# Where a weight buffer lies in 256 bytes: whi 64 bytes before x, wlo at x

## The chip, the cores and the metric

One core of a Trainium2 chip runs the whole program. The metric is the device time of one execution in microseconds (us), as the median of several runs; lower is better. The profile is of one execution on the chip. Its engines are PE (TensorE, matmuls), PEld (the weight loads of the same engine, which overlap the matmuls), DVE (VectorE), ACT (ScalarE), POOL (GpSimd) and SP (SyncE, which issues most DMAs).

## The reference

Two layers of a decoder trunk on x of 256 positions by 2048 features in float32, then a last RMSNorm. Most of the arithmetic is in the projections; the mixers between them are small beside these.

```python
for l in range(DEPTH):                              # DEPTH = 2
    h = rms_norm(x, norm_mix[l])
    proj = h @ w_in[l]                              # 2048 -> 6656
    hq, hf, hi, hg, rq, rk, rv, rg, aq, ak, av = jnp.split(proj, split_at, axis=-1)
    mixed = jnp.concatenate([
        hgrn2_mixer(hq, hf, hi, hg, lb_all[l]),     # gated linear recurrence, 4 heads
        retention_mixer(rq, rk, rv, rg, cos, sin),  # 4 heads
        dilated_attention(aq, ak, av, rel_bias),    # 8 heads, three dilations
    ], axis=-1)
    x = x + mixed @ w_out[l]                        # 2048 -> 2048
    u = rms_norm(x, norm_ffn[l])
    gate = causal_dwconv(u @ w_gate[l], conv_w[l], conv_b[l])   # 2048 -> 5504, width 3
    x = x + (jax.nn.silu(gate) * (u @ w_up[l])) @ w_down[l]     # 5504 -> 2048
return rms_norm(x, norm_final)
```

## The kernel before, in words

**Two parts of each number.** To multiply float32 numbers with the faster float32r matmul, the kernel splits every operand into a first part (hi, the number as ACT writes it in float32r) and a second part (lo, what is left, made by DVE's subtraction). A product is then hi by hi, hi by lo and lo by hi.

**Units.** The weights are cut into units of 128 partitions x 1024 columns (512 KB), 788 in all, walked through in one list. For each unit `dma_unit` (L153) brings the float32 weights into a tile `raw` by a DMA of SP, seven units ahead; `split_unit` (L162) makes `whi` on ACT (recorded at the helper's line, L122) and `wlo` on DVE (L170), three units ahead; `mm_unit` (L173) does the matmuls. `raw` has five buffers in turn, `whi` and `wlo` four each.

**Two modes.** In mode B (w_in in part, w_out, w_gate, w_up, w_down) the weights are stationary, 128 columns at a time, and x streams. A tile of x holds, for each of two blocks of 128 features, 256 columns of hi and then 256 of lo, so the matmul with whi streams all 512 and the one with wlo the first 256. Such two matmuls are called a pair. In mode A (the other part of w_in) a piece of x is stationary and 512 columns of whi or wlo stream, in groups of three matmuls:

```python
# mode B, L202 and L203: out, stationary, streamed
nc.tensor.matmul(o, hi[:, w], x, start=first, stop=False, skip_group_check=True)
nc.tensor.matmul(o[:, 0:S], lo[:, w], x[:, 0:S], start=False, stop=last, skip_group_check=True)
# mode A, L209 to L211
nc.tensor.matmul(o, xh, hi[:, w], start=first, stop=False)
nc.tensor.matmul(o, xh, lo[:, w], start=False, stop=False)
nc.tensor.matmul(o, xl, hi[:, w], start=False, stop=last)
```

Each matmul in the code is two records in the profile: a LDWEIGHTS on PEld, which brings the stationary operand into the array, and a MATMUL on PE, which streams the other one. The x of a unit is in `hp` (the normed x of w_in, w_gate and w_up, built by `build_h`), in `mixp` (the mixers' outputs, for w_out) or in `actp` (the FFN's inner values, for w_down).

**Where the tiles lie.** A pool lays its tags one behind the other in the order in which they are first asked for, each with as many buffers as it has. In `wpool` that is raw, whi, wlo, with 4096 bytes a partition in each buffer. Behind it come `mpool`, which holds all the buffers of x (4096 bytes each, eight for hp, 22 slots that mixp, actp and the mixers' values share, and some smaller tiles of 1024 or 2048), and `const` with xt (4 x 4096), cst (1024), par (1728), masks (1024) and ones (512), in this order. `ones` is the stationary operand of the sums of squares (L273, L1038, L1093).

**Order.** The list of units, and with it the order of PE's matmuls, is written out in `layer`. Small generators (`steps`) put the mixers, the norms and the evacuations between the units; the main loop lets them go on after each unit by about 1.25 us of DVE and 1.3 us of ACT.

Of the kernel before, what the change touches and what calls it, by code (L numbers as in the profile page):

```python
# [10 lines left out]
F32 = mybir.dt.float32  # L11
F32R = mybir.dt.float32r
# [4 lines left out]
P = 128  # L17
# [65 lines left out]
def hybrid_kernel(ctx: ExitStack, tc: tile.TileContext, io):  # L83
    nc = tc.nc

    wpool = ctx.enter_context(tc.tile_pool(name="wpool", bufs=4))
# [33 lines left out]
    def act(out, in_, fn, **kw):  # L120
        want(fn)
        nc.scalar.activation(out, in_, fn, **kw)  # L122
# [30 lines left out]
    def dma_unit(u, parts=1, between=None):  # L153
# [5 lines left out]
                between()  # L159
        raws[u] = t  # L160

    def split_unit(u, parts=1):  # L162
        r = raws.pop(u)
        hi = wpool.tile([P, 1024], F32R, name=f"whi{u}", tag="whi")
        lo = wpool.tile([P, 1024], F32R, name=f"wlo{u}", tag="wlo")
        n = 1024 // parts
        for i in range(parts):
            cs = slice(i * n, (i + 1) * n)
            act(hi[:, cs], r[:, cs], AF.Copy)
            nc.vector.tensor_tensor(lo[:, cs], r[:, cs], hi[:, cs].bitcast(F32), op=OP.subtract)  # L170
        splits[u] = (hi, lo)
# [887 lines left out]
    units = []  # L1059
# [37 lines left out]
    steps.add(first_stats(), 0)  # L1097
    build_h(0, g0)
    split_unit(0, 2)
    dma_unit(3)  # L1100
    build_h(1, g0)
    split_unit(1)
    dma_unit(4)
    xin(6)
    xin(7)
    build_h(2, g0)
    build_h(3, g0)
    split_unit(2)
    dma_unit(5)
    dma_unit(6)  # L1110
# [111 lines left out]
```

## Time and profile before

| | |
|---|---|
| median of 3 runs | 2293.56 us (2293.48 to 2294.77) |
| profiled execution | 2293.8 us, span 2292.0 us |
| granted TensorE clock, mean | 0.997 |
| PE busy | 2267.9 us (99%), 12710 matmuls |
| PEld busy | 1976.2 us (86%), 12710 loads |
| DVE, ACT, POOL busy | 1512.9 us (66%), 1084.1 us (47%), 176.0 us (8%) |
| DMA | 425.10 MB, mean 185 GB/s |

A busy time is the sum of an engine's records. The ends of matmuls are modelled and overlap the next ones, so the rate of PE is read from the starts, not from the busy share. A group row reads: line, engine, operation, out<-in by tile names, shapes, xcount, then the busy us, the mean ns of one, and the engine's idle time just before them with what ended it. A timeline row reads: start and duration in us, engine, line, operation, tiles, shapes, count. A row of one line's instructions reads: the count, the shortest, median and longest duration in ns, and the first and the last start in us. A row of a stretch has its length and then the busy us (and count) of PE, PEld, DVE, ACT and POOL, the clock, the DMA share and GB/s.

### The profile page before, as it was taken

How to read it: one execution, taken by the hardware profiler on the slowest of the kernel's cores; microseconds unless marked ns; L12 is line 12 of the kernel's file. 1: busy time of each engine (PE TensorE's matmuls, PEld its weight loads, DVE VectorE, ACT ScalarE, POOL GpSimd, SP SyncE). 2: the span in 40 equal slices, each digit the busy share in tenths (PEclk: the TensorE clock that was granted, in tenths of full speed). 3: DMA queues.
4: the chain of work that ended last, by engine and by line, in shares of the span. 5: the costliest groups of instructions: out<-in, count | busy, mean ns of one | idle time of the engine just before them, and what ended most of it. 6: DMA issues, size and time to landing. Idle time of an engine off the chain costs nothing.

```text
span 2292.0 us, 32328 instructions
## 1 busy us (share of the span) xinstructions
PE 2267.9 (99%) x12710; PEld 1976.2 (86%) x12710; DVE 1512.9 (66%) x1898; ACT 1084.1 (47%) x1381; POOL 176.0 (8%) x149
## 2 busy tenths in 40 slices
PE   8999999999999999999999999999999999999997
PEld 7888888888888888888888888888888888888886
DVE  5785656777777777555558765577777777765554
ACT  5554544444444444434456444444444444444442
POOL 0250001100000000000012400020000000001111
PEclk9999999999999999999999999999999999999999
DMA  7554455555555555655555455555555555555553
GB/s 256 187 180 166 158 191 177 191 185 193 192 189 189 187 191 188 197 188 189 192 197 180 166 166 175 169 182 197 188 193 187 191 192 190 189 192 190 188 193 110
DMA packets 119587, 425.10 MB, mean 185 GB/s; under 512 B 13411, under 2 KB 16012, under 8 KB 119308
## 3 DMA queue, kind: packets, MB, share of 16 engines
q1 hardware_dynamic: 118412, 420.50, 54.6%
q10 hardware_dynamic: 1024, 2.55, 0.3%
q8 instruction: 100, 1.64, 0.3%
q14 instruction: 51, 0.42, 0.1%
HBM read 420.88 MB, written 3.68 MB: 185 GB/s over the span
## 4 chain that ended last, share of the span: by engine, by line
PE 96%; DVE 2%; POOL 1%; DMA 1%; issue 0%; ACT 0%; DVEq 0%; SPq 0%; POOLq 0%
PE acc L202 54%; PE acc L203 28%; PE acc L209 4%; PE acc L211 4%; PE acc L210 4%; DVE wlo L170 1%; DMA raw<-in_w_b 0%; PE ps_rstd L1093 0%; PE ps_qk L680 0%; DVE rt L760 0%; PE ps_o L710 0%; PE ps_pt L700 0%; PE ps_rs L793 0%; ACT whi L122 0%; POOL hx L488 0%
## 5 line engine op out<-in xcount | busy, mean ns | idle before, releaser
L170 DVE TENSOR_TENSOR wlo<-raw,whi 128x1024 fp32r<-128x1024 f32 (+1 forms) x789 | 998.7, 1269 | 723.7 <-ACT whi L122 717.3
L202 PE MATMUL acc<-hp,whi 128*128 128x512 f32 x3520 | 1230.3, 394 | 7.3 <-ACT whi L122 5.6
L122 ACT ACTIVATE whi<-raw 128x1024 fp32r<-128x1024 f32 (+1 forms) x789 | 831.4, 1056 | 809.7 <-PE acc L202 550.5
L203 PE MATMUL acc<-hp,wlo 128*128 128x256 f32 x3520 | 986.2, 280 | 0.0
L202 PEld LDWEIGHTS acc<-hp,whi 128*128 128x128 f32 x3520 | 660.3, 188 | 155.2 <-ACT whi L122 7.6
L203 PEld LDWEIGHTS acc<-hp,wlo 128*128 128x128 f32 x3520 | 666.4, 189 | 0.6 <-DVE wlo L170 0.4
L202 PE MATMUL acc<-actp,whi 128*128 128x512 f32 x1376 | 477.1, 391 | 0.0
L203 PE MATMUL acc<-actp,wlo 128*128 128x256 f32 x1376 | 385.3, 280 | 0.0
L202 PEld LDWEIGHTS acc<-actp,whi 128*128 128x128 f32 x1376 | 257.3, 187 | 56.4
L203 PEld LDWEIGHTS acc<-actp,wlo 128*128 128x128 f32 x1376 | 260.1, 189 | 0.0
L209 PE MATMUL acc<-whi,hp 128*128 128x512 f32 x448 | 181.0, 404 | 0.0
L202 PE MATMUL acc<-mixp,whi 128*128 128x512 f32 x512 | 178.9, 395 | 0.0
L248 POOL TENSOR_TENSOR sq<-xt 128x512 f32<-128x512 f32 x31 | 33.2, 1071 | 1862.1 <-DVE xt L319 1198.7
L211 PE MATMUL acc<-whi,hp 128*128 128x512 f32 x448 | 175.0, 391 | 0.0
L210 PE MATMUL acc<-wlo,hp 128*128 128x512 f32 x448 | 174.4, 389 | 0.0
L203 PE MATMUL acc<-mixp,wlo 128*128 128x256 f32 x512 | 141.9, 277 | 0.0
L202 PEld LDWEIGHTS acc<-mixp,whi 128*128 128x128 f32 x512 | 96.0, 188 | 21.8
L211 PEld LDWEIGHTS acc<-whi,hp 128*128 128x128 f32 x448 | 84.1, 188 | 18.3
L209 PEld LDWEIGHTS acc<-whi,hp 128*128 128x128 f32 x448 | 84.2, 188 | 16.7
L210 PEld LDWEIGHTS acc<-wlo,hp 128*128 128x128 f32 x448 | 84.3, 188 | 16.6
L203 PEld LDWEIGHTS acc<-mixp,wlo 128*128 128x128 f32 x512 | 96.2, 188 | 0.0
L122 ACT ACTIVATE actp<-up 128x512 fp32r<-128x512 f32 (+1 forms) x44 | 27.4, 623 | 83.3 <-DVE up L849 83.3
(195 smaller groups left out, 1177.4 us busy)
## 6 DMA issues: line engine op xcount, KB each, us to landing
raw<-in_w_d SPq DMA_DIRECT2D x172, 512.0 KB, 3.3
raw<-in_w_g SPq DMA_DIRECT2D x168, 512.0 KB, 3.2
raw<-in_w_u SPq DMA_DIRECT2D x168, 512.0 KB, 3.2
raw<-in_w_a SPq DMA_DIRECT2D x112, 512.0 KB, 3.3
raw<-in_w_b SPq DMA_DIRECT2D x95, 512.0 KB, 3.2
raw<-in_w_out SPq DMA_DIRECT2D x64, 512.0 KB, 3.5
xt<-in_x SPq DMA_DIRECT2D x8, 256.0 KB, 6.6
bias<-brow_d SPq DMA_DIRECT2D x4, 512.0 KB, 4.5
```

Source lines behind the costliest of these rows:

```text
L122: nc.scalar.activation(out, in_, fn, **kw)
L170: nc.vector.tensor_tensor(lo[:, cs], r[:, cs], hi[:, cs].bitcast(F32), op=OP.subtract)
L202: nc.tensor.matmul(o, hi[:, w], x, start=first, stop=False, skip_group_check=True)
L203: nc.tensor.matmul(o[:, 0:S], lo[:, w], x[:, 0:S], start=False, stop=last, skip_group_check=True)
L209: nc.tensor.matmul(o, xh, hi[:, w], start=first, stop=False)
L210: nc.tensor.matmul(o, xh, lo[:, w], start=False, stop=False)
L211: nc.tensor.matmul(o, xl, hi[:, w], start=False, stop=last)
L248: nc.gpsimd.tensor_tensor(sq, x, x, op=OP.mult)
```

## The change

`split_unit` asks for the tiles in another layout. A tile `lead_hi` of 48 floats (192 bytes a partition), which nothing reads or writes, is laid ahead of the buffers of whi, and a tile `lead_lo` of 16 floats (64 bytes) ahead of those of wlo. Each buffer of whi is 1088 floats instead of 1024; the 1024 in use begin at its first float where the unit's mode is B, and 16 floats (64 bytes) further where it is A. Nothing else is changed.

```diff
+    split_leads = []
+
     def split_unit(u, parts=1):
         r = raws.pop(u)
-        hi = wpool.tile([P, 1024], F32R, name=f"whi{u}", tag="whi")
+
+
+        if not split_leads:
+            split_leads.append(wpool.tile([P, 48], F32, name="lead_hi", tag="lead_hi", bufs=1))
+        skip = 0 if units[u][1][0][0].mode == "B" else 16
+        hi = wpool.tile([P, 1024 + 64], F32R, name=f"whi{u}", tag="whi")[:, skip:skip + 1024]
+        if len(split_leads) == 1:
+            split_leads.append(wpool.tile([P, 16], F32, name="lead_lo", tag="lead_lo", bufs=1))
         lo = wpool.tile([P, 1024], F32R, name=f"wlo{u}", tag="wlo")
         n = 1024 // parts
         for i in range(parts):
```

## The prediction

> **What bounds the kernel now.** I read the page's busy times and slices first, then its chain and the waits of the matmul engine, then its groups, and last the timeline and counts of single stretches.
>
> ```profile
> span 2292.0 us, 32328 instructions
> PE 2267.9 (99%) x12710; PEld 1976.2 (86%) x12710; DVE 1512.9 (66%) x1898; ACT 1084.1 (47%) x1381; POOL 176.0 (8%) x149
> PEclk9999999999999999999999999999999999999999
> PE 96%; DVE 2%; POOL 1%; DMA 1%; issue 0%; ACT 0%; DVEq 0%; SPq 0%; POOLq 0%
> ...
> L202 PE MATMUL acc<-hp,whi 128*128 128x512 f32 x3520 | 1230.3, 394 | 7.3 <-ACT whi L122 5.6
> L203 PE MATMUL acc<-hp,wlo 128*128 128x256 f32 x3520 | 986.2, 280 | 0.0
> L202 PE MATMUL acc<-actp,whi 128*128 128x512 f32 x1376 | 477.1, 391 | 0.0
> L203 PE MATMUL acc<-actp,wlo 128*128 128x256 f32 x1376 | 385.3, 280 | 0.0
> L202 PE MATMUL acc<-mixp,whi 128*128 128x512 f32 x512 | 178.9, 395 | 0.0
> L203 PE MATMUL acc<-mixp,wlo 128*128 128x256 f32 x512 | 141.9, 277 | 0.0
> ```
>
> PE is busy for 99% of the span at full clock, makes 96% of the chain, and waits for other engines for a few microseconds in all (7.3 before the largest group). So the time is how fast PE takes its own instructions. Their durations don't tell that: 394 and 280 ns overlap. The spacing of starts does, in a stretch with nothing else on PE:
>
> ```profile
> L203 PE MATMUL acc<-hp,wlo x1154: 280/280/280, 1600.0 to 1999.7; 128*128 128x256 f32 x193
> L203 PE MATMUL acc<-actp,wlo x491: 280/280/280, 2099.9 to 2269.8; 128*128 128x256 f32 x164
> ```
> ```profile
> 1699.84 0.28 PE L203 MATMUL acc<-hp,wlo 128*128 128x256 f32 x1
> 1699.95 0.39 PE L202 MATMUL acc<-hp,whi 128*128 128x512 f32 x1
> 1700.18 0.28 PE L203 MATMUL acc<-hp,wlo 128*128 128x256 f32 x1
> 1700.30 0.39 PE L202 MATMUL acc<-hp,whi 128*128 128x512 f32 x1
> ```
> ```profile
> 1699.84 0.19 PEld L202 LDWEIGHTS acc<-hp,whi 128*128 128x128 f32 x1
> 1699.95 0.19 PEld L203 LDWEIGHTS acc<-hp,wlo 128*128 128x128 f32 x1
> ```
>
> The first row holds 1153 spacings in 399.7 us, 346.7 ns a pair; the second 169.9 / 490, 346.7 again, on other x buffers. A pair is one L202 matmul of 512 columns and one L203 of 256. The timeline splits it: 0.23 us from L202 to L203 and 0.11 to 0.12 (at 230 and 116.7 ns the two make 346.7) from L203 to the next L202. The weight loads start with the matmul before: the load of wlo runs under L202's 512 columns, the load of whi under L203's 256. There are 3520 + 1376 + 512 = 5408 pairs, 5408 x 346.7 ns = 1875 us of the 2292.
>
> How much of it is surplus can be had from a second shape. Where the weights stream instead, three matmuls of 512 columns, each with a load, make a group:
>
> ```profile
> 1227.66 0.39 PE L209 MATMUL acc<-whi,hp 128*128 128x512 f32 x1
> ...
> 1228.34 0.39 PE L209 MATMUL acc<-whi,hp 128*128 128x512 f32 x1
> ```
>
> 0.68 us a group, 226.7 ns a matmul. With c ns a column and f ns a matmul, 512c + f = 226.7 and 768c + 2f = 346.7: f is 2 x (346.7 - 1.5 x 226.7) = 13.3 ns and c 0.417. So each matmul with its load costs some 13 ns beside its columns. That this part isn't a property of the shapes alone is told by another rate on the very same addresses:
>
> ```profile
> 192.01 0.40 PE L202 MATMUL acc<-hp,whi 128*128 128x512 f32 x1
> 192.24 0.28 PE L203 MATMUL acc<-hp,wlo 128*128 128x256 f32 x1
> 192.36 0.40 PE L202 MATMUL acc<-hp,whi 128*128 128x512 f32 x1
> 192.60 0.28 PE L203 MATMUL acc<-hp,wlo 128*128 128x256 f32 x1
> 192.72 0.40 PE L202 MATMUL acc<-hp,whi 128*128 128x512 f32 x1
> 192.96 0.28 PE L203 MATMUL acc<-hp,wlo 128*128 128x256 f32 x1
> 193.07 0.40 PE L202 MATMUL acc<-hp,whi 128*128 128x512 f32 x1
> ```
>
> Here three pairs take 1.06 us, 353.3 ns each, 6.7 more, though nothing waits; the L202 to L203 steps are 0.23, 0.24, 0.24 and the steps back 0.12, 0.12, 0.11. The pattern repeats for some ten microseconds. So a pair's time isn't a property of its shapes alone: how the load and the streamed operand fall against each other in time moves it. That is my reason to think that how they fall in the memory can move it too.
>
> **The change part by part.** Addresses: raw, whi, wlo and the buffers of x (hp, mixp, actp) all have sizes that are multiples of 256 bytes, so today all of them begin at the same place in 256. After it, a 192-byte lead comes ahead of whi and one of 64 ahead of wlo, and each whi is 4352 bytes (17 x 256): whi starts at 192, that is x minus 64, and wlo at 192 + 64 = 256, as x. Where the weights stream (L209 to L211) the view starts 64 bytes in, so whi is as x there.
>
> *Instructions.* None is added, removed or moved: the lead tiles are never written. No DMA, queue or wait changes, 32328 instructions stay. Cost nothing, since there is nothing to hide. The pools grow by 256 + 4 x 256 = 1280 bytes a partition.
>
> *ACT and DVE on whi.* ACT writes whi and DVE reads it, 64 bytes away from raw and wlo.
>
> ```profile
> L170 DVE TENSOR_TENSOR wlo<-raw,whi 128x1024 fp32r<-128x1024 f32 x144 | 176.4, 1225 | 108.9 <-ACT whi L122 106.4
> L122 ACT ACTIVATE whi<-raw 128x1024 fp32r<-128x1024 f32 x145 | 153.3, 1057 | 125.5 <-PE acc L202 93.2 <-issue 20.8 <-ACT conv L122 11.5
> 1600.00:2000.00 400.00, 400.00 (x2309) 352.73 (x2308) 287.97 (x361) 189.70 (x217) 0.00 (x0) 1.00 0.56 190
> ```
>
> Eight pairs, one unit, take 2774 ns of PE; DVE's 1225 and ACT's 1057 for it are made three units ahead. In the stretch DVE is busy 288 of 400 us and ACT 190. I take zero, and even 200 ns more per unit on DVE (144 x 0.2 = 29 us) would leave it below the 400. Were that cover gone, the 5408 / 8 = 676 units of this mode at 0.2 us would be 135 us.
>
> *Streaming weights (L209 to L211).* whi and wlo stay in phase with x: the 226.7 ns stay. Zero, both ways.
>
> *The load of wlo under L202.* Both stay at the same phase, so the 230 ns step stays. Zero, but for what its neighbour hands on.
>
> *The load of whi under L203.* This alone is changed, in 5408 steps of 116.7 ns. No row shows a load of this kind of tile at x minus 64. One tile does lie there: par has 1728 bytes, 64 short of 7 x 256, so ones (after masks of 1024) is at x minus 64, and it is loaded behind L203 and L211:
>
> ```profile
> 1154.50 0.28 PE L203 MATMUL acc<-hp,wlo 128*128 128x256 f32 x1
> 1154.61 0.59 PE L273 MATMUL ps_rstd<-sacc,ones 128*128 128x256 f32 x2
> ```
> ```profile
> 1565.93 0.28 PE L203 MATMUL acc<-hp,wlo 128*128 128x256 f32 x1
> 1566.05 0.59 PE L273 MATMUL ps_rstd<-sacc,ones 128*128 128x256 f32 x2
> ```
>
> 0.11 and 0.12 us: no difference that can be read, but these are single steps into a float32 matmul, not a steady row of float32r ones, and a pair shifts a few ns from one step to the next without a change of its sum. The nearest rows for the steady case are the kernel's own steps from L203 to L202 in a second pattern:
>
> ```profile
> 1500.18 0.39 PE L202 MATMUL acc<-mixp,whi 128*128 128x512 f32 x1
> 1500.41 0.27 PE L203 MATMUL acc<-mixp,wlo 128*128 128x256 f32 x1
> 1500.52 0.40 PE L202 MATMUL acc<-mixp,whi 128*128 128x512 f32 x1
> 1500.76 0.28 PE L203 MATMUL acc<-mixp,wlo 128*128 128x256 f32 x1
> ```
>
> There the step is 0.11, with 0.24 from L202 to L203 in exchange; I read it as 112.5 ns, the middle between 110 and the 115 at which it would be rounded to 0.12. Bounds: at the fast end all 13.3 ns of this one matmul go, 5408 x 13.3 = 72 us less, 2222. At the slow end the 353.3 ns pattern becomes the rule, 5408 x 6.7 = 36 us more, 2330; half of it, a step of 0.12 throughout, is 18 us more, 2312. I take 116.7 - 112.5 = 4.2 ns, the nearest row: the step that the kernel already shows, kept this time instead of exchanged. 5408 x 4.2 = 22.7 us less.
>
> Sum: the profiled execution took 2293.8 us (span 2292.0 and 1.8 around it), 0.2 above the median 2293.56. 2293.8 - 22.7 = 2271.1.
>
> **The rivals.** *Nothing happens.* The 13.3 ns are what a change of weights costs, and a shift of 64 bytes does nothing: 2293.6. For it: 346.7 to four digits on hp and on actp, and the two ones rows; against it: 353.3 ns at 192 us. [...]
>
> *The loads fall into the slow pattern.* A place 64 bytes off leaves the load of whi a little later against L203's columns, the next L202 starts late, and each pair is as at 192 us: 0.24 and 0.12. It decides once the step from L203 to L202 is above 117 ns in the long stretches. Price 36 us if all pairs fall in, 2330; 18 us if half of it, 2312. For it: the pattern exists, and holds itself for ten microseconds. Against it: today's long stretches all leave it within a few units.
>
> *The change gives much more.* Most of the 13.3 ns are a meeting of the two reads, and at x minus 64 they miss each other: down to 2222. For it: the fixed part is the same 13.3 ns in both shapes, and both read at one phase. Against it: the load of ones at x minus 64 shows nothing like it. [...]
>
> **How the numbers follow.** A measurement here tells about 0.2% (4.6 us) from no change; the three runs lie within 1.3 us. Faster 0.46: 0.38 for a part of the 13.3 ns, up to 10 (54 us, 2240), and 0.08 for more than that. Nothing: 0.29. Slower 0.25: 0.17 for up to 18 us, 0.08 above. The forecast is the likeliest, the part, at 2271; its own range is 2240 to 2288. From 2240 to 2312, 0.08 is left out at either end.
>
> **What would show it.** In the changed profile, the L203 count between 1600 and about 2000 us gives the pair: 342.5 ns if right, 346.7 for nothing, 353 for the slow pattern; the timeline there should show 0.11 from L203 to L202 and 0.23 still from L202 to L203; groups of L209 still 0.68 us; DVE's L170 near 1225 ns; 32328 instructions. I am wrong if the L202 to L203 step moves though its load didn't, or if PE begins to wait for whi or wlo.

## The result, and the profile after

The changed kernel took 2257.71 us (median of 4 runs, 2255.88 to 2258.10) against 2293.52 us: a ratio of 0.9842 with a 95% interval of 0.9825 to 0.9859, 35.8 us less. In its listing L202 and L203 (mode B) are L211 and L212, the group L209 to L211 (mode A) is L218 to L220, and L170 is L179. From its page, and from its groups between 1600 and 2000 us:

```profile
span 2255.9 us, 32328 instructions
PE 2232.3 (99%) x12710; PEld 1954.4 (87%) x12710; DVE 1512.4 (67%) x1898; ACT 1083.2 (48%) x1381; POOL 177.9 (8%) x149
PEclk9999999999999999999999999999999999999999
PE 96%; DVE 2%; POOL 1%; DMA 1%; issue 0%; ACT 0%; DVEq 0%; SPq 0%; POOLq 0%
```
```profile
L179 DVE TENSOR_TENSOR wlo<-raw,whi 128x1024 fp32r<-128x1024 f32 x148 | 181.3, 1225 | 103.1 <-ACT whi L122 101.6
L122 ACT ACTIVATE whi<-raw 128x1024 fp32r<-128x1024 f32 x147 | 155.3, 1057 | 121.5 <-PE acc L211 59.7 <-DVE conv L843 30.6 <-issue 20.0
```

The clock (0.997), the instruction counts and the chain's shares are as before (the busy shares of PEld, DVE and ACT are a point higher, as the span is shorter), and DVE's 1225 and ACT's 1057 ns are the same to the nanosecond. What has moved is the pace of PE. The counts of the matmul with wlo, and the timeline (starts in the first column):

```profile
L212 PE MATMUL acc<-hp,wlo x1177: 276/276/276, 1600.0 to 1999.9; 128*128 128x256 f32 x197
L212 PE MATMUL acc<-actp,wlo x471: 276/276/276, 2069.9 to 2229.7; 128*128 128x256 f32 x157
```
```profile
1699.75 0.39 PE L211 MATMUL acc<-hp,whi 128*128 128x512 f32 x1
1699.98 0.28 PE L212 MATMUL acc<-hp,wlo 128*128 128x256 f32 x1
1700.09 0.39 PE L211 MATMUL acc<-hp,whi 128*128 128x512 f32 x1
1700.32 0.28 PE L212 MATMUL acc<-hp,wlo 128*128 128x256 f32 x1
1700.43 0.39 PE L211 MATMUL acc<-hp,whi 128*128 128x512 f32 x1
```

399.9 us over 1176 spacings and 159.8 over 470 are 340.0 ns a pair, where it was 346.7. 5408 pairs times 6.67 ns are 36.1 us, and the span fell by 2292.0 - 2255.9 = 36.1: the whole gain is there. At 192 us, where the kernel before took 353.3 ns a pair, the changed one is at 340 too (1.02 us for three pairs):

```profile
192.21 0.39 PE L211 MATMUL acc<-hp,whi 128*128 128x512 f32 x1
...
193.23 0.39 PE L211 MATMUL acc<-hp,whi 128*128 128x512 f32 x1
```

In mode A, twelve matmuls lie between these two starts, 2.72 / 12 = 226.7 ns each, unchanged:

```profile
1217.70 0.39 PE L220 MATMUL acc<-whi,hp 128*128 128x512 f32 x1
...
1220.42 0.39 PE L220 MATMUL acc<-whi,hp 128*128 128x512 f32 x1
```

### The profile page after: what moved, and what is told of

Read it like the earlier page. It is cut to its first block, busy times and chain, and to the rows that moved or that the text cites. A ratio compares the mean times of both kernels' runs of the same rounds, so it can differ in the third digit from the quotient of the medians.

```text
span 2255.9 us, 32328 instructions
## 1 busy us (share of the span) xinstructions
PE 2232.3 (99%) x12710; PEld 1954.4 (87%) x12710; DVE 1512.4 (67%) x1898; ACT 1083.2 (48%) x1381; POOL 177.9 (8%) x149
## 3 DMA queue, kind: packets, MB, share of 16 engines
q10 hardware_dynamic: 1024, 2.55, 0.4%
## 4 chain that ended last, share of the span: by engine, by line
PE 96%; DVE 2%; POOL 1%; DMA 1%; issue 0%; ACT 0%; DVEq 0%; SPq 0%; POOLq 0%
PE acc L211 54%; PE acc L212 27%; PE acc L218 4%; PE acc L220 4%; PE acc L219 4%; DVE wlo L179 1%; DMA raw<-in_w_b 0%; PE ps_rstd L1102 0%; PE ps_qk L689 0%; PE ps_o L719 0%; DVE rt L769 0%; PE ps_pt L709 0%; PE ps_rs L802 0%; ACT whi L122 0%; POOL hx L497 0%
## 5 line engine op out<-in xcount | busy, mean ns | idle before, releaser
L179 DVE TENSOR_TENSOR wlo<-raw,whi 128x1024 fp32r<-128x1024 f32 (+1 forms) x789 | 998.2, 1269 | 689.8 <-ACT whi L122 686.1
L211 PE MATMUL acc<-hp,whi 128*128 128x512 f32 x3520 | 1206.9, 391 | 7.5 <-DVE hp L243 5.5
L212 PE MATMUL acc<-hp,wlo 128*128 128x256 f32 x3520 | 973.9, 277 | 0.0
L211 PEld LDWEIGHTS acc<-hp,whi 128*128 128x128 f32 x3520 | 662.6, 188 | 146.2 <-ACT whi L122 7.7
L212 PEld LDWEIGHTS acc<-hp,wlo 128*128 128x128 f32 x3520 | 662.7, 188 | 0.6 <-DVE wlo L179 0.4
L211 PE MATMUL acc<-actp,whi 128*128 128x512 f32 x1376 | 467.9, 389 | 0.0
L212 PE MATMUL acc<-actp,wlo 128*128 128x256 f32 x1376 | 379.8, 276 | 0.0
L211 PEld LDWEIGHTS acc<-actp,whi 128*128 128x128 f32 x1376 | 258.3, 188 | 53.8
L212 PEld LDWEIGHTS acc<-actp,wlo 128*128 128x128 f32 x1376 | 258.3, 188 | 0.0
L218 PE MATMUL acc<-whi,hp 128*128 128x512 f32 x448 | 181.0, 404 | 0.0
L211 PE MATMUL acc<-mixp,whi 128*128 128x512 f32 x512 | 175.9, 391 | 0.0
L220 PE MATMUL acc<-whi,hp 128*128 128x512 f32 x448 | 174.9, 390 | 0.0
L212 PE MATMUL acc<-mixp,wlo 128*128 128x256 f32 x512 | 141.5, 276 | 0.0
L211 PEld LDWEIGHTS acc<-mixp,whi 128*128 128x128 f32 x512 | 96.1, 188 | 19.9
L220 PEld LDWEIGHTS acc<-whi,hp 128*128 128x128 f32 x448 | 84.1, 188 | 18.1
L218 PEld LDWEIGHTS acc<-whi,hp 128*128 128x128 f32 x448 | 84.2, 188 | 16.8
L212 PEld LDWEIGHTS acc<-mixp,wlo 128*128 128x128 f32 x512 | 96.2, 188 | 0.0
```

## The experiments

All but two move buffers only: a lead of so many bytes before whi, before wlo and behind wlo, 256 or 512 together, so that x stays where it was in 256 (one run moves x as well). All buffers of weights have 4096 bytes, and there is no shifted view in mode A. In each of them L213 and L214 are the two matmuls of the pair (L217 and L218 in one).

```diff
     def split_unit(u, parts=1):
         r = raws.pop(u)
-        hi = wpool.tile([P, 1024], F32R, name=f"whi{u}", tag="whi")
+        lead(0)      # LEADS[0] bytes, once
+        hi = wpool.tile([P, 1024], F32R, name=f"whi{u}", tag="whi")[:, 0:1024]
+        lead(1)
         lo = wpool.tile([P, 1024], F32R, name=f"wlo{u}", tag="wlo")
+        lead(2)
```

**Is it the 64 bytes at all, and which of the two tiles?** Four kernels. First the changed kernel without its larger buffers and without the shifted view, `LEADS = (192, 64, 0)`:

> whi at x minus 64 in both modes, wlo at x; the buffers of whi keep their 4096 bytes (no 1088-float buffers, no shifted view in mode A). Theory X (the load of whi meets the x streamed by the matmul with wlo): pair 340.0 ns, mode B 36 us below before. Theory L (the loads of whi and wlo, which overlap in time, meet each other): also 340.0. Theory S (the larger buffer pitch, not the 64 bytes): pair 346.7, time as before. In mode A whi now streams at 64 below the stationary x: X and L leave open whether the matmuls there stay at 226.7 ns; if that side of 64 hurts, up to 7 ns x 896 matmuls = 6 us more.

Then wlo alone, `LEADS = (0, 192, 64)`:

> whi at x as before, wlo at x minus 64. Theory X: the load of whi still meets x, so the pair stays at 346.7 ns and the time at 2293, unless the load of wlo under the 512 columns matters too, then 340 or 333. Theory L: the two loads differ by 64, so 340.0 and about 2258.

Both, `LEADS = (192, 0, 64)`:

> whi and wlo both at x minus 64. Theory X: 340.0 ns or less (a further 6.7 ns, 333, if the load of wlo gains as well), 2258 or about 2222. Theory L: the two loads lie alike again, 346.7 and 2293.

And whi on the other side, `LEADS = (64, 192, 0)`:

> whi at x plus 64, wlo at x. If it is only that whi and x (or whi and wlo) must not begin at the same place in 256: 340.0 ns, 2258. If the side counts, because the streamed reads run ahead through the 256 bytes while the load goes on: another value, between 340 and the slow 353.3 ns (2258 to 2330).

The row of the matmul with wlo between 1600 and 2000 us, for these four in order; the pair is the time between the first and the last start over the count less one:

```profile
L214 PE MATMUL acc<-hp,wlo x1177: 276/276/276, 1599.9 to 1999.7; 128*128 128x256 f32 x197
```
```profile
L214 PE MATMUL acc<-hp,wlo x1144: 274/280/285, 1599.7 to 1999.8; 128*128 128x256 f32 x191
```
```profile
L214 PE MATMUL acc<-hp,wlo x1148: 278/280/283, 1599.8 to 2000.0; 128*128 128x256 f32 x192
```
```profile
L214 PE MATMUL acc<-hp,wlo x1143: 281/281/281, 1600.0 to 1999.7; 128*128 128x256 f32 x191
```

340.0, 350.0, 348.9 and 350.0 ns. The ratios to before are 0.9872 (0.9842 to 0.9903), 1.0073 (1.0050 to 1.0096), 1.0096 (1.0066 to 1.0125) and 1.0086 (1.0057 to 1.0115). So the place does it, not the larger buffer (theory S falls). Theory L falls with the second run: the two loads differ by 64 there, and the pair is at 350.0 where the theory gave 340.0. Theory X, that only whi against x counts, falls too: with whi at its good place and wlo 64 lower the pair is at 348.9. And it isn't enough that tiles differ: plus 64 is worse than equal.

Three of these four figures are means of pairs that differ: in the second run the pairs alternate between 346 and 354 ns, in the third they go through about 349, 347 and 351, in the fourth through 352 and 348, over and over. In the first every pair takes 340.

The first of the four also shows what the shifted view is for. In mode A twelve matmuls now take 2.81 us, 234 ns each:

```profile
1222.96 0.40 PE L220 MATMUL acc<-whi,hp 128*128 128x512 f32 x1
...
1225.77 0.40 PE L220 MATMUL acc<-whi,hp 128*128 128x512 f32 x1
```

7.5 ns on 1344 matmuls would be 10 us; the spans of the two kernels differ by 2263.9 - 2255.9 = 8.0, and I expected 6 at most. Over the 1245 steps from one matmul of mode A to the next with nothing between them the mean is 234.1 ns here and 227.9 in the changed kernel, and 6.2 x 1344 = 8.3 us. So the ratio of each of these runs holds a part from mode A as well; the pair is read from mode B alone.

**Is it whi against wlo?** In the four runs and before, 340 came only where whi was 64 below wlo. Four more kernels keep or break that distance, with `LEADS` of (0, 64, 192), (192, 128, 192), (128, 64, 64) and (224, 32, 0):

> whi at x, wlo at x plus 64. So far the pair took 340.0 ns where whi was 64 below wlo (x at wlo), 346.7 and 349 where both were alike, 350.0 where whi was 64 above. Theory D (what counts is whi less wlo, minus 64 being good): 340.0 ns and about 2263, as here too whi is 64 below wlo. Theory X (each load has a place of its own against x; whi wants x minus 64): not 340, about 347 to 350, 2293 to 2312.

> whi at x minus 64, wlo at x plus 64: whi less wlo is minus 128. Theory D gives no number but another one than 340, unless every distance below zero is good; theory X: whi is at its good place, so 340 if wlo above x costs nothing, or 343 if it costs 3.3 ns as wlo at x minus 64 did.

> whi at x minus 128, wlo at x minus 64: whi is again 64 below wlo, both 64 lower against x than in the changed kernel. Theory D: 340.0 ns, about 2263. Theory X: wlo at x minus 64 cost 3.3 ns when alone, so 347 to 353, 2293 to 2330.

> whi at x minus 32, wlo at x: half of the changed kernel's step. If the memory is dealt out in blocks of 64 bytes or more, x minus 32 begins in the same block as x minus 64 and the pair is 340.0 or near; if the time follows the distance smoothly, about 343; if only whole 64 count, 346.7.

```profile
L214 PE MATMUL acc<-hp,wlo x1155: 278/278/281, 1599.9 to 1999.9; 128*128 128x256 f32 x193
```
```profile
L214 PE MATMUL acc<-hp,wlo x1155: 279/279/279, 1599.9 to 1999.9; 128*128 128x256 f32 x193
```
```profile
L214 PE MATMUL acc<-hp,wlo x1155: 279/279/279, 1599.8 to 1999.8; 128*128 128x256 f32 x193
```
```profile
L214 PE MATMUL acc<-hp,wlo x1133: 282/282/282, 1599.8 to 1999.7; 128*128 128x256 f32 x189
```

Three times 400.0 / 1154 = 346.6 (the 346.7 of before, to the rounding of the starts), then 353.3 ns; ratios 1.0016 (1.0005 to 1.0028), 1.0025 (1.0014 to 1.0036), 1.0018 (1.0007 to 1.0030) and 1.0136 (1.0107 to 1.0165). Theory D falls: the first and the third have whi 64 below wlo and gain nothing. The second is at neither number of theory X (340 or 343). Half the step gives the slowest pair of all in this stretch, and none of the three numbers expected: it is neither a smooth slope, nor blocks of 64 bytes, nor whole steps of 64 alone. The few us by which the first three are slower than before, with the same pair, are about what mode A loses: its steps are 231.1 to 231.9 ns on average there, 228.0 before.

**Distances or fixed places, one point or a side?** `LEADS = (192, 64, 0)` with one more lead of 64 bytes ahead of raw, which moves every tile by 64; and `LEADS = (128, 128, 0)`:

> whi at x minus 64 and wlo at x, as in hi_m64_all, but every tile, x too, 64 bytes further on. Theory R (only the distances count): pair 340.0 ns, about 2263. Theory B (fixed blocks of 256 in the memory, against which each tile's own place counts): another value, 347 or more, 2293 or more.

> whi at x minus 128, wlo at x. With wlo at x the pair took 353.3 (whi at minus 32), 346.7 (0), 350.0 (plus 64) and 340.0 (minus 64). If every whole step below x is good: 340.0, about 2263. If minus 64 is one point alone: 346.7 or 350, 2293 to 2312.

```profile
L218 PE MATMUL acc<-hp,wlo x1178: 275/276/277, 1599.8 to 2000.0; 128*128 128x256 f32 x197
```
```profile
L214 PE MATMUL acc<-hp,wlo x1137: 278/282/286, 1600.0 to 1999.9; 128*128 128x256 f32 x190
```

400.2 / 1177 = 340.0 ns (0.9874, 0.9845 to 0.9902) and 399.9 / 1136 = 352.0 ns (1.0122, 1.0093 to 1.0152). Moved together by 64 the tiles give the same pair, so the distances count, not where a tile lies by itself; and minus 128 is no good, slower than either number expected (its pairs go through a cycle of five, from 347 to 359 ns). With wlo at x the pair took 352.0, 340.0, 353.3, 346.7 and 350.0 ns for whi at minus 128, minus 64, minus 32, 0 and plus 64.

**Why minus 64 for the one and 0 for the other?** What tells the two loads apart is what streams while they run: whi's load starts with the 256 columns of the matmul with wlo (in the changed kernel both at 1699.98 us), wlo's with the 512 of the one with whi (1700.10 and 1700.09). Mode A has only 512 columns, with everything at the same place in 256, and its matmuls took 226.7 ns before, two thirds of 340.0. So the matmul with wlo was given 512 columns too:

```diff
-                    nc.tensor.matmul(o[:, 0:S], lo[:, w], x[:, 0:S], start=False, stop=last, skip_group_check=True)
+                    nc.tensor.matmul(o, lo[:, w], x, start=False, stop=last, skip_group_check=True)
```

with whi at x, `LEADS = (0, 0, 256)`, and at x minus 64, `LEADS = (192, 64, 0)`:

> The matmul with wlo streams all 512 columns of x instead of 256 (it adds the product of the two second parts, which the kernel before leaves out); whi and wlo both at x. Theory N (the good place of a load depends on how many columns stream while it runs: x itself under 512, x minus 64 under 256): both loads are now under 512 columns at their good place, 2 x 226.7 = 453.3 ns a pair, so 2293 + 5408 x 106.7 ns = 2870. Theory P (whi wants x minus 64 because of what it is in the order of the pair): 460 ns, about 2906.

> As lo512_p0, with whi at x minus 64. Theory N: the load of whi is now at a bad place under 512 columns, 460 ns or more, about 2906. Theory P: 453.3 ns, about 2864 to 2870.

Between 2100 and 2400 us:

```profile
L214 PE MATMUL acc<-hp,wlo x663: 389/389/389, 2099.6 to 2399.7; 128*128 128x512 f32 x166
```
```profile
L214 PE MATMUL acc<-hp,wlo x654: 387/390/396, 2099.6 to 2400.0; 128*128 128x512 f32 x164
```

300.1 / 662 = 453.3 and 300.4 / 653 = 460.0 ns, 2864.9 and 2905.6 us (ratios 1.2496, 1.2459 to 1.2532, and 1.2673, 1.2636 to 1.2710). Theory N's numbers come out, and theory P falls: the same shift of whi that takes 6.7 ns off a pair when 256 columns stream over its load puts 6.7 on when 512 do.

**Is it ACT, DVE or a DMA that meets whi?** Moving whi moved it against raw and against what ACT and DVE write and read, too. The traces speak against these. Between 1600 and 2000 us of the changed kernel, 459 pairs, each from its start to the start of the next, lie wholly under a DVE instruction with ACT idle, 145 under one of ACT with DVE idle and 56 under both, and all take 340 ns; before, 403, 199 and 64 such pairs all took 346 or 347. And the last two kernels change only what PE streams, with the tiles where the kernel before and the first experiment have them, and turn the sign of the shift around.

## Why the prediction was right, point by point

*What bounds the kernel* was right, and so was the way to read it: the spacing of starts on PE, not the durations. All 36.1 us came from the pair.

*The place of whi against x moves the pair's time* was right, and the reason given, that 346.7 and 353.3 ns on the same addresses can't be a property of the shapes, held. But that reason doesn't say which place is good: nothing in the working picks minus 64. Of the nine places run, one is faster and five are slower by over 0.5%, so that the sign came out was in good part luck. The two patterns are now seen to come and go with the distances: 353.3 is the steady pair with whi at minus 32.

*The term was mis-sized.* "I take 116.7 - 112.5 = 4.2 ns" measured 6.7 ns, 36 us in place of 22.7, so the time lies 13 us below the forecast and inside its range. The step that I took from the second pattern was one half of an exchange between two steps; it doesn't measure what the change takes away.

*"The 230 ns step stays" (the load of wlo)* was wrong. The changed timeline has 0.23 and 0.11 still, but these are rounded: the starts' means over the 1374 pairs in a row on actp are 226.4 and 113.6 ns, from 230.0 and 116.7. The step whose load wasn't moved gave 3.6 ns, the other 3.1. I had said that this would make me wrong, and on this point it does: the two steps can't be charged to a load each, only their sum can be read. The total came out inside the range although the gain was put on one step alone.

*The fixed 13.3 ns* was wrong, and with it the fast end of 2222 and the rival "much more". Its two equations put a shape at its good place (mode A) beside one at a bad place. With both at a good place the same equations leave no fixed part, 2 x (340.0 - 1.5 x 226.7) = 0 to the rounding: 226.7 / 512, 340.0 / 768 and 453.3 / 1024 are all 0.443 ns a column. No run's steady pair fell below that, at any of the places tried.

*"Nothing happens"* fell: by the place of the weights alone the measured times run from 2258 to 2324 us. The two ones rows that the prediction put down for it (0.11 and 0.12 us) were single steps into a float32 matmul, and told nothing of a steady row.

*The slow rival* came true at other places: five of the eight others tried have a ratio above 1.005, up to 353.3 ns a pair, and 32 bytes in place of 64 would have made this change slower. Its reason isn't borne out: it put the loss on the step from the matmul with wlo to the next with whi, and with whi at minus 32 that step has 117.5 ns on actp (116.7 before), the other 235.8 (230.0).

*The edits costed at nothing* (ACT, DVE, pools, mode A) cost nothing; that mode A's zero hangs on the shifted view, 8 us of span, the prediction did not price.

What stays open is the mechanism below this: whether it is reads that meet and which, and why 256 and 512 columns want places that differ by 64 bytes. Theory N is shown at two column counts and two places of whi only, and the runs with 512 columns lengthen the whole pair as well as the stream over that one load, which isn't told apart. The runs do show that neither load can be judged alone, and that one kernel can have two patterns at the same distances (346.7 and 353.3 ns before). Only distances below 256 bytes were varied by the leads; the changed kernel's buffers of whi lie 4352 bytes apart and those of the first experiment 4096, and both give 340.0, so whole steps of 256 make no difference there. Most other places of whi, in steps of 32, and other column counts weren't tried.

## What to carry to other kernels

Where PE is busy throughout (99% of the span here), take the spacing of matmul starts over a long steady stretch and divide it by the streamed columns: two shapes with a different rate a column (before, 346.7 / 768 = 0.451 ns in mode B and 226.7 / 512 = 0.443 in mode A) are a hint that one of them loses time to something, here to where its weights lie. It is a hint only: a fixed cost of each matmul, which the prediction read out of it, would look the same. Then move the buffers by leads of 64 bytes and read the spacing again in one profile each; over the 1153 spacings before, starts given to 0.1 us leave about 0.1 ns, where the four totals of the changed kernel lie between 2255.88 and 2258.10 us. Find the place anew for each column count and each role, as a good place for one was a bad one for the other (whi at x minus 64: 340.0 in place of 346.7 ns a pair with 256 columns over its load, 460.0 in place of 453.3 with 512, and 234 in place of 226.7 ns a matmul in mode A).

## What the runs showed of the hardware that I had not expected

- A pair of float32r matmuls of 512 and 256 columns, each with a load of 128 x 128, takes 340.0 to 353.3 ns on average over 400 us on hp by where the three tiles lie to each other in 256 bytes. Of the places tried, 340.0 was reached only with whi at x minus 64 and wlo at x, and there also with all tiles 64 bytes further on.
- At some places the pairs repeat in a cycle: 346 and 354 ns in turn with wlo alone at x minus 64, a cycle of five pairs from 347 to 359 with whi at minus 128.
- Moving a tile by 32 bytes changes the pair by 6.7 ns and more: 346.7, 353.3 and 340.0 for whi at 0, minus 32 and minus 64.
- The best rate seen in these float32r matmuls is 0.443 ns a column, in matmuls of 512 columns (mode A, and the pair of 512 and 512) and in the pair of 512 and 256.
- In mode A, whi streamed at 64 below the stationary x makes the matmuls 234 in place of 226.7 ns.
